# A decoder step's stalls: rope's copies first, low parts moved between engines, and later weights, gates and taps

## The chip, the cores and the metric

The kernel runs on one core of one Trainium2 chip. A core has five engines, each with its own instruction queue: TensorE (PE: matmuls; PEld: its weight loads), VectorE (DVE), ScalarE (ACT), GpSimd (POOL), and SyncE (SP), which here starts all DMA transfers. They share the on-chip memory SBUF; matmuls write to PSUM. The metric is the time of one execution in microseconds (us), as the median of three runs.

## The reference

One layer of a decoder with three parallel branches, for a prompt of 1024 positions and 8 samples of 4 positions (together 1056 columns), in float32:

```python
h = rmsnorm(x, norm_mix_g)
q, k, v, g, su, sv, xq, gt = split(h @ w_in)
o_ret, S = retention(rope(q), rope(k), v, silu(g))        # 4 heads, group norm
o_sg  = gelu(su) * (tril(sg_ws) @ layernorm(gelu(sv)) + sg_bs)
o_x   = softmax(xq @ mk.T) @ mv                           # 256 memory tokens
merged = sig(gA) * (o_ret @ w_br_ret) + sig(gB) * (o_sg @ w_br_sg) + sig(gC) * (o_x @ w_br_x)
x = x + merged @ w_o
z = rmsnorm(x, norm_ffn_g) @ w_up                         # 1024 -> 2 x 2816
a, b = split(conv_b + causal depthwise convolution of width 3 over z)
x = x + (gelu(a) * b) @ w_down
y = rmsnorm(x, norm_final_g)
```

Model width is 1024. States of the retention and the convolution and the normalised gate rows are returned too.

## The kernel before, in words

Activations lie feature-major: a tile is 128 features by 1056 columns. Each matmul is computed in three terms: both operands are split into a high part (rounded to float32r) and a low part (the rest), and high x high, high x low and low x high are summed in PSUM.

Weights come as slabs of 128 x 1024 (the list SLABS gives their order). `w_prep` makes one ready: its DMA lands in wr, ScalarE casts it to wh (whs in the down projection), and GpSimd subtracts to get wl (wls); for the slabs in the set LO_DVE, VectorE subtracts instead (`vtt` is VectorE's two-tensor operation, `ptt` is GpSimd's). There are three buffers of wh and wl. `w_ahead` calls `w_prep` if a buffer is free.

A unit `fm` computes one output tile of 128 features in 8 k-steps of nine matmuls (three terms by three column chunks), into one PSUM tile, mp. After each k-step it calls `hook`. A hook pops functions due from the list `wait` (filled by `later(n, fn)`: run fn n hooks from now), one entry of a side list, and, by a `rate` of steps per hook, advances generators that hold secondary work: norms, the retention, attention, convolutions. Every engine works off its queue in the order in which the code issues; that order is set by these hooks and rates, written by hand. An instruction that reads a PSUM tile is also ordered behind earlier readers of it.

The places that the change touches:

- **Start.** `xnorm` sums the squares of x (tiles xr) over k = 4 to 7 on ScalarE, YA hooks after it begins, adds them on VectorE, and `rstd_all` splits the sum into rsh and rsl, sums over features with matmuls (ap<-rsh, ap<-rsl) and forms rst. Meanwhile q and k of head 0 are projected together, and the silu gate behind them needs rst.
- **Rope.** `rope_evac` takes q's or k's PSUM tile: VectorE multiplies by the cosines, ScalarE copies the two halves swapped into sw, GpSimd multiplies sw by sines, and VectorE adds. In heads 1 to 3 this falls among the retention of the head before, whose group norm uses GpSimd for a tiny reciprocal root (grs) between VectorE's mv and cB; ort follows from them.
- **Spatial gate and cross-attention.** su, sgt and sgS belong to the spatial gate. In cross-attention, KS splits a head's cached keys (kch, kcl), QS its queries (xqh, xql), XA to YC are scores, softmax and products (xt, pt).
- **Gates.** `gate` projects one tile of a gate; calling what it returns runs the tanh (th) and stores it.
- **Output projection.** wo runs in two halves of 528 columns, eight slabs each (L1534 calls `w_ahead`). During the second half the first is normalised (ns, nst, rst, `h_scale` into x2c, xl) and sums of up weights (fs) are formed.
- **Up projection.** The up projection's second pair uses 2x2 products; `z_put` assembles z, and a convolution has `first`, `tap(1)`, `tap(0)`, `gelu`.
- **Down projection.** Groups of two slabs; in each, eight outputs m of 18 matmuls are added to x; the last convolution's steps run at `rate[0]` per output. acl is an activation's low part.
- **Tail.** The last two groups are computed by column chunks of 512, 288 and 256 (c = 0, 1, 2). `fin_evac` adds to x, squares (sq), and adds to ssf; `fin(c)` casts ssf to sy, sums over features (ap<-sy), gets rsy, and multiplies into y; `fin_last` does it for c = 2, where the squares of m = 6, 7 go straight into float32 matmuls.

In the program `H` is 4, `NFF` 22, `NUP` 44.

Of the kernel before, what the change touches and what calls it, by code (L numbers as in the profile page):

```python
# [75 lines left out]

LO_DVE = [k for i, k in enumerate(SLABS) if k[0] in ("km", "vm") and i % 2] + [("sv", 0, 0), ("sv", 0, 1)]


@with_exitstack  # L80
def step_kernel(ctx: ExitStack, tc: tile.TileContext, xT, memT, wslab, cst, ident_d, rope, vec, sgc, sgm, sgs,
# [10 lines left out]
    def slot(name, dt=F32, shape=None):  # L92
        return sp.tile(shape or [P, T], dt, tag="S", name=name, bufs=NSLOT)
# [31 lines left out]
    def psv(ps):  # L125
        return [ps[:, 0:2, 0:384], ps[:, 2, 0:288]]

    def seg(t):
        return [t[:, 0:768].rearrange("p (a b) -> p a b", a=2), t[:, 768:1056]]
# [101 lines left out]
    def fm(key, ops, kbase=0, free=True):  # L231
        hi, lo = w_get(key)
        hv = hi.rearrange("p (k c) -> p k c", c=P)
        lv = lo.rearrange("p (k c) -> p k c", c=P)
        ps = mp()
        n = len(ops)
        for k in range(n):
            rh, rl = ops[k]
            for i, (a, r) in enumerate(((hv, rh), (hv, rl), (lv, rh))):
                for c, (c0, w) in enumerate(CH):  # L240
                    mm(ps[:, c, 0:w], a[:, kbase + k, :], r[:, c0:c0 + w],
                       start=(k == 0 and i == 0), stop=(k == n - 1 and i == 2))
            if k == 0 or k == 3:
                w_ahead()
            hook()
        if free:
            w_free(key)
        return ps
# [107 lines left out]
    with tc.manual_schedule():  # L356
# [72 lines left out]

        YA, YB = 14, 3  # L430

# [43 lines left out]
        def rope_evac(ps, name):  # L475
            sw = slot("sw")
            out = slot(name)
            for o, i, c in zip(seg(out), psv(ps), seg(cosT)):
                vtt(o, i, c, ALU.mult)
            for (a, b) in ((0, 64), (64, 0)):  # L480
                for o, i in zip(seg(sw), psv(ps)):
                    nc.scalar.copy(out=o[a:a + 64], in_=i[b:b + 64])
            ptt(sw, sw, sinT, ALU.mult)
            later(4, lambda: vtt(out, out, sw, ALU.add))
            return out
# [459 lines left out]
        def xattn(h):  # L945
# [134 lines left out]
            for fn, *a in ((XA, 0), (YA, 0), (XA, 1), (YA, 1), (XB, 0), (VS, 0), (XB, 1), (XC, 0), (VS, 1), (XA, 2), (YB,),  # L1080
                           (XC, 1), (XB, 2), (XA, 3), (YC, 0), (XC, 2), (KS, h + 1, 0), (XB, 3), (YC, 1),
                           (KS, h + 1, 1), (XC, 3), (QS, h + 1), (YD,)):
                while defer:
                    defer.pop(0)()
                fn(*a)
                if fn not in (VS, KS, QS):
                    yield
# [211 lines left out]
        for m in range(8):  # L1299
            if m == 6:  # L1300
                side.extend([g_load] * 8)
            if m == 7:
                side.extend([lambda k=k: g_scale(k) for k in range(8)])
            gate(("gb", m))()
        drain()
# [430 lines left out]
        vtt(za[1][:, :, 2:6], za[1][:, :, 2:6], by4(u4[:, 2 * HA:HW]), ALU.add)  # L1736
        pb.first()
        pb.tap(1)
        conv = [Conv(1, *za), Conv(NFF + 1, *zb)]
        n = prod(d["a22"], "T4", tick=do)  # L1740
        z_put(n, 0, *zb, u3)
        pb.tap(0)
        conv_end(0, pa, pb)
# [98 lines left out]
        gens.append(last_conv())  # L1842
        rate[0] = 1.0

# [19 lines left out]
        def down(g):  # L1864
            ws = dn_get(g)
            tr = terms(g, ws)
            for m in range(8):
# [4 lines left out]
                for o, i in zip(seg(x2t[m]), psv(ps)):  # L1872
                    vtt(o, o, i, ALU.add)
                if m in (1, 3, 5):
                    w_ahead()
# [15 lines left out]
        rsy = slot("rsy")  # L1891
        sy3 = slot("sy3", F32R)
        FCH = ((0, 512), (512, 288), (800, 256))

        def fin(c):
            c0, w = FCH[c]
            r = rsy[:, c0:c0 + w]
            yield
            yield from rstd_cols(ssf[:, c0:c0 + w], w, r, sy3, fine=True)
            for m in range(0, 8, 2):  # L1900
                y = slot("y", shape=[P, 2, 512])
                for i in range(2):
                    ptt(y[:, i, 0:w], x2t[m + i][:, c0:c0 + w], r, ALU.mult)
                later(2, lambda m=m, y=y: dma(yT[m:m + 2, :, c0:c0 + w].rearrange("m p t -> p m t"), y[:, :, 0:w]))
                yield

        def fin_last(sqs):
# [3 lines left out]
            a = ap()[:, 0:w]  # L1911
            mm(a, ones, sy3[:, 0:w], stop=False)
            mm(a, ones, sy3[:, w:2 * w], start=False, stop=False)
            for i in range(2):
                mm(a, f(ones), sqs[i], start=False, stop=(i == 1))
            t = slot("rn")
# [19 lines left out]
        def fin_evac(c, us, pss):  # L1936
# [8 lines left out]
            for m in us:  # L1945
                if c == 2 and m > 5:
                    last_sq.append(sqs[m])
                elif m:
                    vtt(ssf[:, sl], ssf[:, sl], sqs[m], ALU.add)
            if c == 2 and us[-1] == 5:  # L1950
                nc.scalar.copy(out=sy3[:, 0:w], in_=ssf[:, sl])
                vtt(sy3[:, w:2 * w], ssf[:, sl], f(sy3[:, 0:w]), ALU.subtract)
            for m in us:
# [176 lines left out]
```

## Time and profile before

| | us |
|---|---|
| median of three runs | 1917.12 (1916.0 to 1917.32) |
| the profiled execution | 1916.06 |
| its span, first to last instruction | 1913.9 |
| TensorE busy | 1854.7 |
| VectorE busy | 1144.7 |
| GpSimd busy | 921.5 |
| ScalarE busy | 651.8 |

The mean clock that TensorE was granted is 0.991 of full. Of the 2.2 us between the span and the execution's time nothing is seen in the trace. Rows of instructions read: start in us, duration in us, engine, line of the code, operation, out<-in, shapes, count, and in brackets the engine's idle time before it and what ended that. The count x3 means three instructions one behind the other, with one duration from the start of the first to the end of the last. Rows of waits read: the instructions that waited, what they waited for, then the sum in us, how often, and the longest.

### The profile page before, as it was taken

How to read it: one execution, taken by the hardware profiler on the slowest of the kernel's cores; microseconds unless marked ns; L12 is line 12 of the kernel's file. 1: busy time of each engine (PE TensorE's matmuls, PEld its weight loads, DVE VectorE, ACT ScalarE, POOL GpSimd, SP SyncE). 2: the span in 40 equal slices, each digit the busy share in tenths (PEclk: the TensorE clock that was granted, in tenths of full speed). 3: DMA queues.
4: the chain of work that ended last, by engine and by line, in shares of the span. 5: the costliest groups of instructions: out<-in, count | busy, mean ns of one | idle time of the engine just before them, and what ended most of it. 6: DMA issues, size and time to landing. Idle time of an engine off the chain costs nothing.

```text
span 1913.9 us, 32100 instructions
## 1 busy us (share of the span) xinstructions
PE 1854.7 (97%) x13369; PEld 1828.0 (96%) x13369; DVE 1144.7 (60%) x1610; ACT 651.8 (34%) x1016; POOL 921.5 (48%) x583
## 2 busy tenths in 40 slices
PE   8899999999999999999999999899999999999997
PEld 8899999999999998999999999899999999999996
DVE  6554545442464479332352267999999999744447
ACT  6333232421233434323211233544344344321204
POOL 2243434221643421555544533577777777754404
PEclk9999999999999999999999999999999999999998
DMA  5112131324133341426632532022222223732202
GB/s 189 54 45 93 44 105 36 132 66 156 56 135 112 124 181 55 135 90 255 241 124 79 189 140 84 34 90 79 68 90 79 67 90 120 252 133 90 76 1 91
DMA packets 59808, 204.82 MB, mean 107 GB/s; under 512 B 6608, under 2 KB 9840, under 8 KB 59664
## 3 DMA queue, kind: packets, MB, share of 16 engines
q1 hardware_dynamic: 59664, 202.78, 30.8%
q8 instruction: 105, 1.72, 0.4%
q14 instruction: 39, 0.32, 0.1%
HBM read 154.34 MB, written 48.41 MB: 106 GB/s over the span
## 4 chain that ended last, share of the span: by engine, by line
PE 50%; DVE 7%; issue 1%; ACT 1%; POOL 1%; DMA 1%; DVEq 0%; SPq 0%; POOLq 0%; ACTq 0%
PE bp L108 25%; PE mp L108 25%; DVE c L120 1%; DVE xl L114 1%; DVE x2c L120 1%; DVE fs L114 1%; DVE ssf L114 0%; DMA opr<-scr 0%; POOL opl L117 0%; DMA wr<-in_wslab 0%; DVE x L114 0%; ACT xh L1153 0%; DVE hx L114 0%; POOL acl L117 0%; POOL wls L117 0%
## 5 line engine op out<-in xcount | busy, mean ns | idle before, releaser
L117 POOL TENSOR_TENSOR wl<-wr,wh 128x1024 fp32r<-128x1024 f32 x107 | 282.7, 2645 | 438.3 <-ACT wh L152 294.7
L108 PE MATMUL bp<-xh,wh 128*128 128x264 f32 (+1 forms) x1376 | 279.2, 284 | 6.8 <-DVE th L114 2.4
L108 PE MATMUL bp<-xh,wl 128*128 128x264 f32 (+1 forms) x1376 | 280.3, 285 | 1.2 <-POOL wl L117 0.7
L108 PE MATMUL bp<-xl,wh 128*128 128x264 f32 (+1 forms) x1376 | 279.8, 285 | 0.0
L108 PEld LDWEIGHTS bp<-xh,wh 128*128 128x128 f32 x1376 | 215.0, 189 | 8.2 <-issue 3.1
L108 PEld LDWEIGHTS bp<-xh,wl 128*128 128x128 f32 x1376 | 215.0, 189 | 1.8 <-POOL wl L117 1.2
L108 PEld LDWEIGHTS bp<-xl,wh 128*128 128x128 f32 x1376 | 214.5, 189 | 0.0
L108 PE MATMUL mp<-hh,wh 128*128 128x384 f32 (+1 forms) x816 | 190.0, 340 | 4.9 <-ACT hh L111 4.8
L108 PE MATMUL mp<-hl,wh 128*128 128x384 f32 (+1 forms) x816 | 179.6, 327 | 0.3 <-DVE hl L120 0.3
L114 DVE TENSOR_TENSOR x<-x,mp 128x288 f32<-128x288 f32 (+3 forms) x167 | 105.7, 676 | 120.6 <-PE mp L108 120.6
L108 PE MATMUL mp<-hh,wl 128*128 128x384 f32 (+1 forms) x816 | 177.6, 324 | 0.0
L117 POOL TENSOR_TENSOR wl<-fs,wh 128x1024 fp32r<-128x1024 f32 x52 | 146.2, 2814 | 50.9 <-ACT wh L1179 50.4
L108 PEld LDWEIGHTS mp<-hh,wh 128*128 128x128 f32 x816 | 136.0, 191 | 7.8 <-ACT hh L111 5.4
L108 PEld LDWEIGHTS mp<-hl,wh 128*128 128x128 f32 x816 | 136.6, 190 | 1.1 <-DVE hl L120 1.0
L108 PEld LDWEIGHTS mp<-hh,wl 128*128 128x128 f32 x816 | 137.0, 189 | 0.0
L108 PE MATMUL mp<-ach,whs 128*128 128x384 f32 (+3 forms) x524 | 124.3, 326 | 4.0 <-DVE x L114 3.1
L120 DVE SCALAR_TENSOR_TENSOR c<-z,hist,c 128x1024 f32<-128x1024 f32 x88 | 125.0, 1420 | 4.3 <-ACT c L111 4.2
L108 PE MATMUL mp<-ach,wls 128*128 128x384 f32 (+3 forms) x524 | 123.7, 325 | 0.0
L108 PE MATMUL mp<-acl,whs 128*128 128x384 f32 (+3 forms) x524 | 123.4, 325 | 0.0
L152 ACT CAST wh<-wr 128x1024 fp32r<-128x1024 f32 x86 | 89.4, 1043 | 95.8 <-PE mp L108 54.2
L1179 ACT CAST wh<-fs 128x1024 fp32r<-128x1024 f32 x55 | 57.7, 1050 | 155.6 <-DVE fs L114 145.3
L120 DVE SCALAR_TENSOR_TENSOR c<-zs,hist,c 128x32 f32<-128x32 f32 x88 | 110.6, 1256 | 0.0
(367 smaller groups left out, 4161.5 us busy)
## 6 DMA issues: line engine op xcount, KB each, us to landing
wr<-in_wslab SPq DMA_DIRECT2D x162, 512.0 KB, 3.7
sg<-th SPq DMA_DIRECT2D x24, 528.0 KB, 5.2
th<-sg SPq DMA_DIRECT2D x24, 528.0 KB, 5.5
sca<-c SPq DMA_DIRECT2D x22, 528.0 KB, 3.0
opr<-sca SPq DMA_DIRECT2D x22, 528.0 KB, 4.7
opr<-scr SPq DMA_DIRECT2D x16, 528.0 KB, 7.0
scr<-ort SPq DMA_DIRECT2D x8, 528.0 KB, 7.6
hx<-in_xT SPq DMA_DIRECT2D x8, 528.0 KB, 5.9
```

Source lines behind the costliest of these rows:

```text
L108: nc.tensor.matmul(out=out, lhsT=l, rhs=r, start=start, stop=stop)
L114: nc.vector.tensor_tensor(out=out, in0=a, in1=b, op=op)
L117: nc.gpsimd.tensor_tensor(out=out, in0=a, in1=b, op=op)
L120: nc.vector.scalar_tensor_tensor(out=out, in0=a, scalar=s, in1=b, op0=op0, op1=op1)
L152: nc.scalar.copy(out=hi, in_=raw)
L1179: nc.scalar.copy(out=hi, in_=src)
```

## The change

- `LO_DVE` also holds the second half of wo and xq 2 and 3: their low parts are made by VectorE.
- `fm` calls `w_ahead` after its second and fifth k-step instead of the first and fourth.
- At the start, YA is 11 instead of 14. `rope_evac` copies sw before the multiplication in head 0; in the other heads GpSimd's multiplication is issued two hooks later, and the addition five hooks later instead of four.
- In cross-attention the next head's QS comes before its second KS.
- The tanh and store of gate gb run two hooks later.
- In the up projection's second pair `first` and `tap(1)` come behind the last `z_put`.
- In the down groups the rate is 0.34 instead of 1, and group 0 has no `w_ahead` at m = 1.
- In the tail, chunk 1 begins its norm two hooks later; four y of chunk 0 are VectorE's; chunk 2 casts ssf into a tile of its own, sy4, after m = 2, and the squares of m = 3 to 7 go into float32 matmuls.

```diff
 LO_DVE = [k for i, k in enumerate(SLABS) if k[0] in ("km", "vm") and i % 2] + [("sv", 0, 0), ("sv", 0, 1)]
+LO_DVE += [("wo", m, 1) for m in range(8)]
+LO_DVE += [("xq", 2), ("xq", 3)]
...
-            if k == 0 or k == 3:
+            if k == 1 or k == 4:
                 w_ahead()
...
-        YA, YB = 14, 3
+        YA, YB = 11, 3
...
         def rope_evac(ps, name):
             sw = slot("sw")
             out = slot(name)
+            def turn():
+                for (a, b) in ((0, 64), (64, 0)):
+                    for o, i in zip(seg(sw), psv(ps)):
+                        nc.scalar.copy(out=o[a:a + 64], in_=i[b:b + 64])
+
+            if h == 0:
+                turn()
             for o, i, c in zip(seg(out), psv(ps), seg(cosT)):
                 vtt(o, i, c, ALU.mult)
-            for (a, b) in ((0, 64), (64, 0)):
-                for o, i in zip(seg(sw), psv(ps)):
-                    nc.scalar.copy(out=o[a:a + 64], in_=i[b:b + 64])
-            ptt(sw, sw, sinT, ALU.mult)
-            later(4, lambda: vtt(out, out, sw, ALU.add))
+            if h:
+                turn()
+            if h:
+                later(2, lambda: ptt(sw, sw, sinT, ALU.mult))
+            else:
+                ptt(sw, sw, sinT, ALU.mult)
+            later(5 if h else 4, lambda: vtt(out, out, sw, ALU.add))
             return out
...
-                           (KS, h + 1, 1), (XC, 3), (QS, h + 1), (YD,)):
+                           (QS, h + 1), (KS, h + 1, 1), (XC, 3), (YD,)):
...
-            gate(("gb", m))()
+            later(2, gate(("gb", m)))
...
-        pb.first()
-        pb.tap(1)
         conv = [Conv(1, *za), Conv(NFF + 1, *zb)]
         n = prod(d["a22"], "T4", tick=do)
         z_put(n, 0, *zb, u3)
+        pb.first()
+        pb.tap(1)
         pb.tap(0)
...
         gens.append(last_conv())
-        rate[0] = 1.0
+        rate[0] = 0.34
...
-                if m in (1, 3, 5):
+                if m in ((3, 5) if g == 0 else (1, 3, 5)):
                     w_ahead()
...
-        sy3 = slot("sy3", F32R)
+        sy3, sy4 = slot("sy3", F32R), slot("sy4", F32R)
...
-            yield
+            for _ in range(3 if c else 1):
+                yield
             yield from rstd_cols(ssf[:, c0:c0 + w], w, r, sy3, fine=True)
...
-                    ptt(y[:, i, 0:w], x2t[m + i][:, c0:c0 + w], r, ALU.mult)
+                    (vtt if c == 0 and m < 4 else ptt)(y[:, i, 0:w], x2t[m + i][:, c0:c0 + w], r, ALU.mult)
...
-            mm(a, ones, sy3[:, 0:w], stop=False)
-            mm(a, ones, sy3[:, w:2 * w], start=False, stop=False)
-            for i in range(2):
-                mm(a, f(ones), sqs[i], start=False, stop=(i == 1))
+            mm(a, ones, sy4[:, 0:w], stop=False)
+            mm(a, ones, sy4[:, w:2 * w], start=False, stop=False)
+            for i in range(len(sqs)):
+                mm(a, f(ones), sqs[i], start=False, stop=(i == len(sqs) - 1))
...
-                if c == 2 and m > 5:
+                if c == 2 and m > 2:
                     last_sq.append(sqs[m])
...
-            if c == 2 and us[-1] == 5:
-                nc.scalar.copy(out=sy3[:, 0:w], in_=ssf[:, sl])
-                vtt(sy3[:, w:2 * w], ssf[:, sl], f(sy3[:, 0:w]), ALU.subtract)
+            if c == 2 and us[-1] == 2:
+                nc.scalar.copy(out=sy4[:, 0:w], in_=ssf[:, sl])
+                vtt(sy4[:, w:2 * w], ssf[:, sl], f(sy4[:, 0:w]), ALU.subtract)
```

The changed program's line numbers are some two higher near the helpers. On ScalarE, at the start of the program, from q's last copies sw to the cast rsh, before (xr<-xr are the squares, two pairs):

```order
L482 COPY sw<-mp 64x768
L482 COPY sw<-mp 64x288
L152 CAST wh<-wr 128x1024
L111 ACTIVATE xr<-xr 128x1056 x2
L482 COPY sw<-mp 64x768
L482 COPY sw<-mp 64x288
L482 COPY sw<-mp 64x768
L482 COPY sw<-mp 64x288
L152 CAST wh<-wr 128x1024
L111 ACTIVATE xr<-xr 128x1056 x2
L337 CAST rsh<-xr 128x1056
```

On ScalarE from the same copies to the same cast, now:

```order
L483 COPY sw<-mp 64x768
L483 COPY sw<-mp 64x288
L154 CAST wh<-wr 128x1024
L113 ACTIVATE xr<-xr 128x1056 x2
L483 COPY sw<-mp 64x768
L483 COPY sw<-mp 64x288
L483 COPY sw<-mp 64x768
L483 COPY sw<-mp 64x288
L154 CAST wh<-wr 128x1024
L339 CAST rsh<-xr 128x1056
```

The pair that stands here now is the second; the first stands ahead of q's copies, and nothing but a weight's cast is left between k's copies and rsh.

On GpSimd, in head 2's rope of k among the retention of head 1 (grs are the group norm's two small operations), before:

```order
L117 TENSOR_TENSOR grs<-mv,cB 128x1
L117 TENSOR_TENSOR grs<-grs,nhalf 128x1
L117 TENSOR_TENSOR sw<-sw,sinT 128x1056
L117 TENSOR_TENSOR wl<-wr,wh 128x1024
L117 TENSOR_TENSOR grs<-mv,cB 128x1
L117 TENSOR_TENSOR grs<-grs,nhalf 128x1
```

On GpSimd at the same place, now:

```order
L119 TENSOR_TENSOR grs<-mv,cB 128x1
L119 TENSOR_TENSOR grs<-grs,nhalf 128x1
L119 TENSOR_TENSOR grs<-mv,cB 128x1
L119 TENSOR_TENSOR grs<-grs,nhalf 128x1
L119 TENSOR_TENSOR wl<-wr,wh 128x1024
L119 TENSOR_TENSOR sw<-sw,sinT 128x1056
```

The second pair of grs moved ahead of sw and wl, and sw moved behind wl.

On VectorE, in the second half of wo, from one output's addition to the next (x2c<-mp,x2c adds an output, fs are sums of up weights), before:

```order
L120 SCALAR_TENSOR_TENSOR x2c<-mp,x2c 128x528
L114 TENSOR_TENSOR ssq<-ssq,sq 128x528
L114 TENSOR_TENSOR fs<-fr 128x512
L114 TENSOR_TENSOR fs<-fs,fr 128x512
L120 SCALAR_TENSOR_TENSOR x2c<-x2c,vecs,rst 128x528
L114 TENSOR_TENSOR xl<-x2c,xh 128x528
L120 SCALAR_TENSOR_TENSOR x2c<-x2c,vecs,rst 128x528
L114 TENSOR_TENSOR xl<-x2c,xh 128x528
L120 SCALAR_TENSOR_TENSOR x2c<-mp,x2c 128x528
```

On VectorE at the same place, now:

```order
L122 SCALAR_TENSOR_TENSOR x2c<-mp,x2c 128x528
L116 TENSOR_TENSOR ssq<-ssq,sq 128x528
L116 TENSOR_TENSOR fs<-fr 128x512
L116 TENSOR_TENSOR fs<-fs,fr 128x512
L116 TENSOR_TENSOR wl<-wr,wh 128x1024
L122 SCALAR_TENSOR_TENSOR x2c<-x2c,vecs,rst 128x528
L116 TENSOR_TENSOR xl<-x2c,xh 128x528
L122 SCALAR_TENSOR_TENSOR x2c<-x2c,vecs,rst 128x528
L116 TENSOR_TENSOR xl<-x2c,xh 128x528
L122 SCALAR_TENSOR_TENSOR x2c<-mp,x2c 128x528
```

One wl per output came in ahead of the next addition; it was GpSimd's before.

## The prediction

> **What bounds the kernel now.** I read the page's busy times first, then the list of TensorE's waits, then busy time and granted clock in the stretches where the long waits lie, and last the rows of the engines that end those waits.
>
> ```profile
> PE 1854.7 (97%) x13369; PEld 1828.0 (96%) x13369; DVE 1144.7 (60%) x1610; ACT 651.8 (34%) x1016; POOL 921.5 (48%) x583
> ```
>
> TensorE is the bound: of the span of 1913.9 us it leaves 59.2 idle. A change that leaves its matmuls alone (this one adds three small ones at the end) can win those 59 us and what a reduced clock costs, no more. The first column after the colon is the sum in us, then how often, then the longest:
>
> ```profile
> PE ap L108 <- ACT rsh L337: 5.9, 1, 5.9
> ...
> PE ap L108 <- DVE ort L120: 3.7, 3, 2.9
> PE mp L108 <- DVE x L114: 3.1, 2, 2.6
> PE ap L108 <- DVE sgt L114: 3.0, 1, 3.0
> PE mp L108 <- DVE x2c L120: 2.7, 2, 2.0
> ...
> PE bp L108 <- DVE z L114: 2.1, 1, 2.1
> PE ap L108 <- DVE xql L114: 2.1, 1, 2.1
> PE ap L108 <- ACT sy L319: 1.9, 1, 1.9
> PE ap L108 <- DVE ns L114: 1.7, 1, 1.7
> PE ap L108 <- DVE pt L114: 1.6, 3, 0.9
> PE mp L108 <- DVE silu L114: 1.5, 1, 1.5
> PE ap L108 <- ACT xt L111: 1.3, 1, 1.3
> ...
> PE bp L108 <- POOL wl L117: 0.7, 1, 0.7
> ```
>
> Nearly every row is one wait at one place, and each part of the change touches one of these places. The last row says that weights are practically never late. The stretches (PEclk is the granted clock):
>
> ```profile
> core 0: us, PE busy (x) PEld busy (x) DVE busy (x) ACT busy (x) POOL busy (x), PEclk, DMA share, GB/s
> 45.00:56.00 11.00, 4.51 (x15) 3.98 (x15) 7.74 (x6) 3.88 (x4) 5.17 (x13) 0.69 0.23 54
> 223.00:230.00 7.00, 4.06 (x18) 3.63 (x17) 3.83 (x8) 0.47 (x1) 2.40 (x3) 0.76 0.25 75
> 527.00:534.00 7.00, 4.04 (x18) 3.76 (x18) 6.74 (x7) 0.00 (x0) 2.21 (x1) 0.76 0.74 235
> 593.00:597.00 4.00, 3.60 (x25) 3.57 (x26) 2.59 (x8) 1.02 (x4) 0.00 (x0) 1.00 0.90 259
> 1120.00:1160.00 40.00, 35.62 (x277) 35.04 (x276) 34.87 (x36) 16.53 (x24) 15.51 (x6) 0.96 0.30 100
> 1227.00:1245.00 18.00, 14.79 (x107) 14.40 (x106) 17.93 (x21) 6.73 (x13) 9.37 (x11) 0.91 0.17 60
> 1653.00:1660.00 7.00, 4.41 (x19) 4.16 (x18) 7.00 (x7) 2.02 (x2) 7.00 (x3) 0.76 0.58 181
> 1888.00:1896.00 8.00, 5.56 (x32) 5.15 (x31) 7.00 (x12) 3.56 (x9) 6.54 (x5) 0.79 0.47 176
> ```
>
> A long wait is paid twice: in 223 to 230 the mean clock is 0.76, so (1-0.76) x 7.00 = 1.7 us of TensorE's time is lost to the clock after a wait of 2.9; 1.7 again after sgt and x, 1.7 after sy, 1.6 after x2c (0.04 x 40) and z (0.09 x 18). After xql (2.1, stretch 593 to 597) the clock stays 1.00: the wait must lie badly for it. I count 1.5 for each window, since part of one is idle.
>
> The Trainium skill ("TensorE: Matmul & The Clock Gate", Why this matters for your kernels) asks only that idle gaps between matmuls stay under about 3 us; by it, only the 5.9 us wait would cost clock here, and the sum below would be smaller by five windows x 1.5 = 7.5 us. The stretches above, with waits of 1.9 to 3.0 us and a clock of 0.76 to 0.79, speak against it, and I go by them.
>
> **Part by part** (gains positive).
>
> *Start.*
>
> ```profile
> 29.53 2.19 ACT L482 COPY sw<-mp 64x768 f32<-64x768 f32 x4 [5.15 <-DVE q L114]
> 32.70 2.06 ACT L111 ACTIVATE xr<-xr 128x1056 f32<-128x1056 f32 x2
> 44.34 5.52 DVE L114 TENSOR_TENSOR xr<-xr 128x1056 f32<-128x1056 f32 x3 [4.19 <-ACT xr L111]
> 55.91 0.64 PE L108 MATMUL mp<-hh,wh 128*128 128x384 f32 x3
> 56.39 0.65 PE L108 MATMUL mp<-hl,wh 128*128 128x384 f32 x3
> ```
>
> The squares of the first norm wait on ScalarE behind the rope copies sw, and these wait for VectorE's multiplication q, though they need only the PSUM tile. The change lets the first pair of squares run in the 5.15 that ScalarE idled, and copies before it multiplies, so that sw starts at about 27.7 (an estimate: 29.53 less the multiplication). The second pair followed sw's start by 32.70 - 29.53 = 3.17, so it runs from 30.9 to 33.0. xr's three sums, 1.84 each beside GpSimd (5.52 / 3), end at 38.5, the cast rsh (1.1) at 39.6; rsl stands behind k's multiplication and q's addition on VectorE (together 2.5), and ends at 42.3 (40.8 to 43.5).
>
> TensorE's summing matmuls stand three k-steps earlier. A k-step is three triples, 3 x (56.39 - 55.91) = 1.45, so they come at about 40.7 instead of 45.1, where the wait began (51.0 - 5.9). The copies now hold the multiplication up, but its tile is needed again only two outputs later. So 5.9, 1.5 (silu, which the same chain makes late) and 2.0 of clock go: in 45 to 56 the clock lost (1-0.69) x 11.00 = 3.4, part of it while TensorE stood. Of the 9.4, a new wait of 0 to 2.5, taken as 1.4, comes back. Gain 8 (6 to 10).
>
> *Rope in heads 1 to 3.*
>
> ```profile
> 219.90 2.47 POOL L117 TENSOR_TENSOR sw<-sw,sinT 128x1056 f32<-128x1056 f32 x1 [4.66 <-ACT sw L482]
> 222.31 2.39 POOL L117 TENSOR_TENSOR wl<-wr,wh 128x1024 fp32r<-128x1024 f32 x1
> 224.64 0.21 POOL L117 TENSOR_TENSOR grs<-mv,cB 128x1 f32<-128x1 f32 x1
> ```
>
> The group norm's tiny grs stands behind sw and wl on GpSimd; behind it on VectorE wait cB and ort, and TensorE 2.9 for ort. In head 2 grs now stands ahead of both: 2.9 + 1.5 clock = 4.4. In heads 1 and 3 the second grs stays behind both, and wl starts later, its cast now behind the copies: grs about 1.1 us later, 0.8 lost in each (0 to 2). Gain 2.8 (0.4 to 4.4).
>
> *xq's low parts on VectorE.*
>
> ```profile
> 523.79 5.98 DVE L114 TENSOR_TENSOR su<-su,sgt 128x512 f32<-128x512 f32 x1
> 524.54 4.67 POOL L117 TENSOR_TENSOR wl<-wr,wh 128x1024 fp32r<-128x1024 f32 x2
> L114 DVE TENSOR_TENSOR wl<-fs,wh x3: 1225/1226/1256, 728.3 to 764.0; 128x1024 fp32r<-128x1024 f32 x3
> ```
>
> A VectorE operation on two SBUF tiles that meets one on GpSimd lasts until that is done: su took 5.98. With both wl on VectorE, at 1.23 each as the last row shows for such tiles, su meets none, but a wl of 1.23 may stand ahead of the next sgt: that follows about 2 us earlier. The wait of 3.0 shrinks to 0.9, the clock window goes: gain 3.5 (1 to 4.5).
>
> The Trainium skill ("Perfetto Trace Analysis", Optimizing Scalar/DVE Operations) warns that VectorE and GpSimd share a port, so moving operations between these two might not help; by it this term and wo's below would be 0, and the sum 6.5 smaller. The rows have a price for both sides, 1.23 on VectorE against a wait of 2.4 per wl, so I keep the terms, and make the warning a rival.
>
> *QS ahead of the second KS.* xqh's cast moves ahead of another tile's; xql, for which TensorE waits 2.1 without loss of clock, is ready before it is needed. Gain 2.0 (1 to 2.1). The key halves behind it come one step later; they are used a head later.
>
> *gb gates two hooks later.*
>
> ```profile
> 695.83 1.18 ACT L111 ACTIVATE th<-th,vecs 128x1056 f32<-128x1056 f32 x1 [4.14 <-DVE th L114]
> ```
>
> In this stage the attention of the xq heads runs between the gates' k-steps, and a gate's tanh of 1.18 stands ahead of pt's casts and xt's exponentials on ScalarE. Behind them it delays only its own store on SP's queue, which is read back a stage later. The waits for xt (1.3) and pt (1.6) are the ones it can shorten: 2.9 at best; since other casts stay ahead of them, I take half. Gain 1.5 (0 to 2.9).
>
> *wo's second half, low parts on VectorE.*
>
> ```profile
> 1122.27 2.45 DVE L114 TENSOR_TENSOR ns<-ssq,ns 128x528 fp32r<-128x528 f32 x1 [0.76 <-ACT ns L1476]
> ```
>
> ns took 2.45 because a wl ran on GpSimd. Without the eight wl's there, ns' wait of 1.7 shrinks to 0.6, x2c's 2.7 to 1.0, and the window's 1.5 goes: 4.3. But VectorE is busy 34.87 of 40 here, and gets 8 x 1.23 = 9.8 for the locked time it loses, and a wl stands ahead of ns. I take 3.0 (-1 to 6).
>
> *Second up pair.* z is written 1.3 earlier, but VectorE is busy 17.93 of 18 in that stretch, so what TensorE gains on z it waits for at zu. -0.4 (-2 to 1.5).
>
> *Down groups.* Taps at 0.34 per hook instead of 1: VectorE, full from 1653 to 1660 (7.00 of 7.00), has x earlier. The 3.1 and the window's 1.5 go; three taps that meet GpSimd's low parts leave about 0.35 each, and one weight less ahead costs nothing, as the row for wl in the waits says (if that cover is gone, one slab's 2.4). Gain 3.6 (1 to 4.6).
>
> *Tail.*
>
> ```profile
> 1884.10 3.71 DVE L114 TENSOR_TENSOR ssf<-ssf,sq 128x288 f32<-128x288 f32 x3
> 1897.21 6.86 POOL L117 TENSOR_TENSOR y<-x,rsy 128x288 f32<-128x288 f32 x8 [2.67 <-DVE rsy L120]
> 1899.37 2.36 DVE L114 TENSOR_TENSOR ssf<-ssf,sq 128x256 f32<-128x256 f32 x3
> ```
>
> The column sum's two matmuls of chunk 1 now stand 30 matmuls later, among chunk 2's second group, so sy's wait of 1.9 and its window go, 3.4. Ahead of that sy, though, VectorE gets four y of 0.7 to 1.2 (the ssf additions beside GpSimd took 3.71 / 3), of which about 1.5 comes back as a rest of the wait. In the last group the additions (2.36) leave the path for three pairs of small matmuls beside x: some 1.5 more. Against it, rsy of chunk 1 comes behind x of chunk 2, so GpSimd's eight y (6.86) now run beside the last norm and the last six y on VectorE and stretch them, or end last themselves, about 2. Left are 3.4 - 1.5 + 1.5 - 2 = 1.4, taken as 1.5 (-2 to 4.5).
>
> The sum: 8 + 2.8 + 3.5 + 2.0 + 1.5 + 3.0 - 0.4 + 3.6 + 1.5 = 25.5. A removed wait uncovers another: behind the 5.9 stood 1.5 (silu). I take 3 off, an eighth, for those the rows do not show yet. 22.5 against the profiled execution's own 1916.06 gives 1893.6; the median stands 1.06 higher: 1894.6.
>
> **Rivals.**
>
> *Shared-port swaps give nothing.* wo, xq and the tail only exchange a wait on GpSimd for work on VectorE, and each window stays. Then 3.0 + 3.5 + 1.5 is missing: a gain of 14.5, 1902.6. For it: VectorE's 34.87 of 40; against it: su's 5.98, of which two wl of 1.23 would use 2.5. This is the case of the warning in the Trainium skill's "Perfetto Trace Analysis" above.
>
> *Rests still trip the clock.* At four places (start, wo, down, tail) a wait near 1.9 remains and the window with it: 4 x (1.5 + 0.5) = 8 lost (0.5 for the longer rest), 1902.6 likewise. Against it: 2.1 for xql tripped nothing.
>
> *Nothing uncovered, and the ends reached.* Without the 3 taken off, and with the upper ends of start (2 more) and wo (3 more): 1917.1 - 25.5 - 5 = 1886.6. For it: most waits stand alone, microseconds from the next; against it: silu behind rsh.
>
> *Slower: weights late.* Every feature-major unit now prepares its next weights one k-step (1.45 us) later.
>
> ```profile
> L117 POOL TENSOR_TENSOR wl<-wr,wh 128x1024 fp32r<-128x1024 f32 x107 | 282.7, 2645 | 438.3 <-ACT wh L152 294.7
> ```
>
> If the low part were the last thing that a unit waits for, each of the 56 units (56 calls over the loops of heads, gates and branches) would lose up to 1.45. At 22.5 / 56 = 0.40 each it takes all that the rest wins, and at 0.5 each the time is 1894.6 + 28 = 1922.6. Against it: TensorE waited for wl 0.7 us in all, and GpSimd idled 438.3 ahead of those 107.
>
> **How the numbers follow.** Forecast (1887 to 1901) 0.64; swaps give nothing 0.13; rests trip the clock 0.08; the better ends 0.07; slower 0.04; nearly nothing left, by several new waits of the size of the old, 0.04. The time is the forecast's. The range reaches to 1886.5 below, the better end, and to 1904 above, just past the two rivals at 1902.6. 0.2% is 3.8 us, about what a measurement of this kernel tells from no change. Faster 0.93, same 0.03, slower 0.04.
>
> **What would show it.** rsh's wait under 2.5; ort, sgt, xql, x at 1657 and sy gone from the long waits, and clock 1.00 in those stretches; su at 0.7 to 2; ns at 0.7; TensorE's idle time near 37 us, not 59. The prediction is wrong if wl or wh appear among TensorE's waits with more than 5 us, if x2c or zu wait longer than 3, or if GpSimd's y is the last work.

## The result, and the profile after

The changed kernel takes 1896.23 us (median of four runs, 1894.87 to 1897.33) against 1916.56 for the kernel before (median of four); the ratio is 0.9894, 95% interval 0.9877 to 0.9911. The forecast was 1894.6, range 1886.5 to 1904.0. The profiled execution took 1896.17 with a span of 1894.2, 19.7 less than before.

The page's busy times after:

```profile
PE 1845.7 (97%) x13375; PEld 1821.7 (96%) x13375; DVE 1137.5 (60%) x1621; ACT 652.0 (34%) x1016; POOL 906.1 (48%) x569
```

TensorE stands idle 48.5 us instead of 59.2, and its busy time fell by 9.0 with six matmul records more (two for each of the three small matmuls): that part is clock, not work. The mean granted clock rose from 0.991 to 0.995. TensorE's waits after:

```profile
PE mp L110 <- DVE x L116: 5.2, 4, 1.6
PE ap L110 <- ACT rsh L339: 3.2, 1, 3.2
PE ap L110 <- DVE ort L122: 2.9, 2, 1.5
...
PE bp L110 <- DVE zt L116: 2.3, 1, 2.3
PE ap L110 <- DVE rsl L116: 1.8, 1, 1.8
PE mp L110 <- DVE x2c L122: 1.3, 2, 0.9
...
PE bp L110 <- POOL wl L119: 0.7, 1, 0.7
...
PE ap L110 <- DVE ns L116: 0.5, 1, 0.5
...
PE ap L110 <- ACT sy L321: 0.2, 1, 0.2
...
PE ap L110 <- DVE sgt L116: 0.2, 1, 0.2
```

xql is gone from the list, sgt, sy and ns shrank to 0.5 or less; ort's 2.9 is two waits of 1.5 and 1.4 instead of one long one, zt's 2.3 is new, and rsh and rsl still stand for 5.0. Stretches of the same stages after, with the granted clock in the column PEclk:

```profile
41.00:56.00 15.00, 10.28 (x49) 9.88 (x50) 10.76 (x11) 6.24 (x7) 2.85 (x2) 0.77 0.14 37
...
210.00:230.00 20.00, 20.00 (x133) 19.59 (x132) 14.35 (x29) 5.19 (x10) 7.00 (x8) 1.00 0.09 27
520.00:534.00 14.00, 13.77 (x100) 13.38 (x99) 13.46 (x18) 2.14 (x3) 3.82 (x2) 1.00 0.58 193
1105.00:1145.00 40.00, 38.15 (x310) 37.56 (x309) 32.35 (x43) 18.72 (x26) 3.90 (x2) 1.00 0.34 110
1205.00:1227.00 22.00, 18.35 (x132) 17.51 (x131) 21.93 (x22) 9.56 (x18) 13.20 (x12) 0.92 0.18 71
1630.00:1640.00 10.00, 10.00 (x64) 10.00 (x63) 7.77 (x11) 4.93 (x5) 6.59 (x4) 1.00 0.32 107
...
1865.00:1878.00 13.00, 10.31 (x81) 9.46 (x80) 10.79 (x21) 6.44 (x16) 5.08 (x4) 1.00 0.44 163
```

Five of the seven stretches of reduced clock are whole; the start (0.77) and the up pair (0.92) are not. Where the time came from is read by matching each matmul with itself in the other trace. Its start before less its start after is TensorE's lead there, in us:

| before the matmul at (us, before) | lead | gained in the stage | forecast |
|---|---|---|---|
| 72.0, behind the start | 1.6 | 1.6 | 8 |
| 399.9, behind heads 1 to 3 | 4.1 | 2.5 | 2.8 |
| 560.0, behind the spatial gate | 8.1 | 4.0 | 3.5 |
| 759.6, behind attention and gb | 14.9 | 6.8 | 3.5 |
| 1180.0, behind wo | 18.9 | 4.0 | 3.0 |
| 1300.1, behind the second up pair | 18.2 | -0.7 | -0.4 |
| 1870.1, behind the down groups (lead 18.0 at 1610) | 19.5 | 1.5 | 3.6 |
| end of the span | 19.7 | 0.2 | 1.5 |

A lead also moves where nothing was changed. The first matmul starts anywhere from 4.8 to 5.7. The seven traces with the changed kernel's start (its own, e4, e5, e6, e8, e9, e12) lie up to 1.0 apart at 70 us; two of the experiments (e8, e12) lost 1.2 in the up pair, and one (e6) 1.8 in the down groups, without an edit there. In the experiments, too, a lead is that of one trace over another, and a cost is the change of the lead across the stage that was edited. Spans are of one profiled execution each, unless an interval is given; the changed kernel's is 1894.2, and its four executions have 1892.9 to 1895.4.

### The profile page after: what moved, and what is told of

It reads as the page before. It is cut to its first block, busy times and chain, and to the rows that moved or that the text cites. A ratio compares the mean times of both kernels' runs of the same rounds, so it can differ in the third digit from the quotient of the medians.

```text
span 1894.2 us, 32097 instructions
## 1 busy us (share of the span) xinstructions
PE 1845.7 (97%) x13375; PEld 1821.7 (96%) x13375; DVE 1137.5 (60%) x1621; ACT 652.0 (34%) x1016; POOL 906.1 (48%) x569
## 4 chain that ended last, share of the span: by engine, by line
PE 52%; DVE 7%; ACT 1%; issue 1%; POOL 1%; DVEq 0%; ACTq 0%
PE bp L110 26%; PE mp L110 25%; DVE c L122 2%; DVE xl L116 1%; DVE x2c L122 1%; DVE fs L116 0%; DVE wl L116 0%; DVE x L116 0%; DVE hx L116 0%; POOL opl L119 0%; DVE z L116 0%; ACT xh L1164 0%; DVE ssf L116 0%; DVE c L116 0%; ACT sq L113 0%
## 5 line engine op out<-in xcount | busy, mean ns | idle before, releaser
L119 POOL TENSOR_TENSOR wl<-wr,wh 128x1024 fp32r<-128x1024 f32 x97 | 258.4, 2666 | 424.6 <-ACT wh L154 284.6
```

Of the source, the lines that this page charges most:

```text
L119: nc.gpsimd.tensor_tensor(out=out, in0=a, in1=b, op=op)
```

## The experiments

### Where the start's gain went

The first undoes the start alone.

```diff
-        YA, YB = 11, 3
+        YA, YB = 14, 3
...
-            if h == 0:
-                turn()
             for o, i, c in zip(seg(out), psv(ps), seg(cosT)):
                 vtt(o, i, c, ALU.mult)
-            if h:
-                turn()
+            turn()
```

> The changed kernel with the start as before (YA 14, copies behind the multiplication in head 0). Theory A (the start part gave little, since the three additions of xr now lie beside four GpSimd operations in a row and took 9.77 us instead of 5.52): the three waits at the start are 5.9, 0.6 and 1.5 again, TensorE is 1.5 to 2.5 us later from 70 us on than in the changed kernel, and the span is about 1896 (1894.2 + 1.6 to 2.5). Rival B (the start part is worth the 8 us forecast, and something else in the changed kernel, such as the weights prepared a k-step later, loses 6 there): TensorE is some 8 us later from 70 us on, span about 1902.

The waits at the start were 5.9, 0.6 and 1.5 again, TensorE was 2.4 later at 70 us, and the span was 1896.9. Theory A stands: the start was worth 2.4 in this pair of traces and not 8. (Set against all seven traces with the new start, the kernel before and e1 give 0.7 to 2.4.) The rows of VectorE and then of GpSimd in the changed kernel show why:

```profile
33.02 9.77 DVE L116 TENSOR_TENSOR xr<-xr 128x1056 f32<-128x1056 f32 x3 [1.72 <-ACT xr L113]
...
32.45 2.41 POOL L119 TENSOR_TENSOR wl<-wr,wh 128x1024 fp32r<-128x1024 f32 x1
35.28 3.05 POOL L119 TENSOR_TENSOR sw<-sw,sinT 128x1056 f32<-128x1056 f32 x1 [0.41 <-ACT sw L483]
38.28 3.38 POOL L119 TENSOR_TENSOR wl<-wr,wh 128x1024 fp32r<-128x1024 f32 x1
```

The three additions begin at 33.0, as forecast, but each lies beside one of GpSimd's operations, and they take 2.96, 3.43 and 3.31: 9.77 for three, where the forecast took the 5.52 of before. Of those 5.52 only the first addition lay beside GpSimd, and this is its row:

```profile
44.34 2.93 DVE L114 TENSOR_TENSOR xr<-xr 128x1056 f32<-128x1056 f32 x1 [4.19 <-ACT xr L111]
```

The other two took 1.26 each. If so, taking one operation off GpSimd must bring rsh forward.

```diff
+LO_DVE += [("g", 1)]
```

> The changed kernel with one more low part made by VectorE: that of the silu gate's second slab, the first of the two that GpSimd makes beside the additions of xr. Theory A: GpSimd's row then has the two sw and one wl, the additions start beside nothing, the last ends with the second sw at about 37.8, rsh at about 39; TensorE's wait of 3.2 for rsh goes, that for rsl (1.8) shrinks under 1, the clock stays 1.00: 5 to 7 us less, span 1887 to 1889. Rival B (the squares and copies set rsh, not GpSimd): rsh comes at most 1 us earlier and the span stays within 1.5 us of 1894.2.

VectorE, then TensorE, in this run:

```profile
33.89 5.99 DVE L117 TENSOR_TENSOR xr<-xr 128x1056 f32<-128x1056 f32 x3
39.80 1.31 DVE L117 TENSOR_TENSOR k<-mp,cosT 128x768 f32<-128x768 f32 x2
41.03 2.20 DVE L117 TENSOR_TENSOR q<-q,sw 128x1056 f32<-128x1056 f32 x1
...
44.45 0.45 PE L111 MATMUL ap<-rsl,ones 128*128 128x384 f32 x1 [2.97 <-DVE rsl L117]
```

The additions take 5.99 (1.24, 1.26 and, beside sw, 3.42), the wait for rsh is gone, the clock stays at 1.00 from 40 to 50 us, and the span is 1889.9, 4.3 less. The mechanism of A is shown; the size fell short of 5, because rsl, behind q's addition (2.20, stretched as well), now waits 3.0 and not under 1. Moving the next slab's low part as well helps no more:

```diff
+LO_DVE += [("g", 1), ("v", 0, 0)]
```

> As the run before, and the next slab's low part (v of head 0) also by VectorE, where it stands ahead of rsl. Theory A: additions as before or shorter by up to 1 us, rsh at 39 or earlier, but rsl about 1.2 later than in the run before, so a wait of 1 to 2 for rsl: span 0 to 2 us above that run's. Rival B: the span stays within 1.5 us of 1894.2.

Span 1892.0, 2.1 above e2, of which 1.0 stands from the first matmuls on. The low part stands ahead of rsl, whose wait is 3.2 and not the 1 to 2 of theory A, and in 41 to 56 the clock is 0.89, where e2 has 1.00.

### The rope, and the weights a k-step later

```diff
-            if h:
+            if h == 2:
                 later(2, lambda: ptt(sw, sw, sinT, ALU.mult))
...
-            later(5 if h else 4, lambda: vtt(out, out, sw, ALU.add))
+            later(5 if h == 2 else 4, lambda: vtt(out, out, sw, ALU.add))
```

> The changed kernel with sw's multiplication and the addition put off in head 2 alone; heads 1 and 3 as before. Theory A (putting off helps where grs stood behind sw, and loses 1.0 and 1.1 in heads 1 and 3, where it still stands behind wl, which starts later): the waits for ort in heads 1 and 3 are about 0.4 instead of 1.5 and 1.4, head 2 has none, span 2.1 lower, about 1892. Rival B (weights prepared a k-step later make the 1.5 in heads 1 and 3, whatever sw does): both waits stay at 1.4 to 1.5 and the span at 1894.

The waits for ort in heads 1 and 3 did fall to 0.4 and 0.3, but a wait for st of 0.7 and 0.9 appeared earlier in each, where sw now delays another norm. The lead over the changed kernel changed by less than 0.2 in each head, and the span is 1894.1: A was right on ort and wrong on the sum. Then the step of the weights alone was undone:

```diff
-            if k == 1 or k == 4:
+            if k == 0 or k == 3:
                 w_ahead()
```

> The changed kernel with weights prepared after the first and fourth k-step again. Theory A (the shift costs nothing, since weights are ready long ahead, and wins a little where it puts a cast behind others on ScalarE): span 0 to 2.5 higher, no wait for wl over 1 us in either. Rival B (the later weights cost in heads 1 and 3, where grs waits behind a wl that starts later): the waits for ort in heads 1 and 3 fall from 1.5 and 1.4 to about 0.4, span about 2 lower.

Both theories fell: the span is 1905.6, 11.4 more. TensorE is 1.3 later at 110 us, 3.1 at 140, 10.6 at 240, 12.4 at 400 and 13.1 at 560; from there to 700 it makes up 1.7. So nearly all of it is lost in heads 1 to 3. ort is waited for 2.1, 4.0 and 2.0, and the clock is 0.77 over 225 to 240:

```profile
PE ap L110 <- DVE ort L122: 8.1, 3, 4.0
```

ScalarE, GpSimd and VectorE in head 2 of that run:

```profile
223.35 1.05 ACT L154 CAST wh<-wr 128x1024 fp32r<-128x1024 f32 x1
224.30 0.36 ACT L538 COPY cB<-ap 128x256 f32<-128x256 f32 x1
...
224.47 2.38 POOL L119 TENSOR_TENSOR wl<-wr,wh 128x1024 fp32r<-128x1024 f32 x1 [5.73 <-ACT wh L154]
226.81 0.19 POOL L119 TENSOR_TENSOR grs<-mv,cB 128x1 f32<-128x1 f32 x1
227.08 0.55 POOL L119 TENSOR_TENSOR grs<-grs,nhalf 128x1 f32<-128x1 f32 x1
227.59 2.40 POOL L119 TENSOR_TENSOR sw<-sw,sinT 128x1056 f32<-128x1056 f32 x1
...
227.66 2.48 DVE L541 TENSOR_SCALAR cB<-cB,mv,grs 128x256 f32<-128x256 f32 x1 [5.75 <-POOL grs L119]
```

Without the later step the cast wh is issued ahead of the norm's copy cB, so that wl stands ahead of grs on GpSimd. sw, put off by two hooks, now starts just when VectorE uses grs, and stretches that operation as well (2.48). In the changed kernel the same operation takes 0.41, and wl and sw follow it:

```profile
220.31 0.41 DVE L541 TENSOR_SCALAR cB<-cB,mv,grs 128x256 f32<-128x256 f32 x1 [1.91 <-ACT cB L538]
221.24 2.39 POOL L119 TENSOR_TENSOR wl<-wr,wh 128x1024 fp32r<-128x1024 f32 x1 [1.95 <-ACT wh L154]
```

The later cast is not a neutral edit: it takes wl from in front of the norm. Is it enough by itself? One run had the rope of heads 1 to 3 as before, with the weights kept later, and three edits elsewhere:

```diff
+LO_DVE += [("g", 1)]
...
-            if h:
-                later(2, lambda: ptt(sw, sw, sinT, ALU.mult))
-            else:
+            if 1:
                 ptt(sw, sw, sinT, ALU.mult)
-            later(5 if h else 4, lambda: vtt(out, out, sw, ALU.add))
+            later(4 if h else 7, lambda: vtt(out, out, sw, ALU.add))
...
-        rate[0] = 0.34
+        rate[0] = 0.25
```

> The changed kernel with the silu gate's second low part by VectorE (as in e2), q's addition in head 0 put behind rsl (7 hooks instead of 4), the rope of heads 1 to 3 as before the change (with the weights still prepared a k-step later), and taps at 0.25 per output in the down groups. Theory A, start: rsl ends 1 to 1.5 sooner than in e2, where q's addition of 2.2 stood ahead of it, so 1 to 1.5 more than e2's 4.2. Theory A, rope: the later weights alone take wl out of the group norm's way in head 2 (ScalarE's copy of cB goes ahead of the cast), and sw's move adds nothing there: head 2's wait for ort stays under 0.6, heads 1 and 3 as in e4, so the same time within 0.5. Rival B, rope: sw's 2.5 ahead of grs is what counts, the wait in head 2 is 2 or more, and with a reduced clock 2 to 4 are lost there. Down groups: at 0.25 one tap less lies beside GpSimd's low parts, 0 to 1.5 earlier at 1690. Span under theory A 1887 to 1889.5.

Rope: rival B holds. GpSimd, VectorE and TensorE in head 2:

```profile
216.98 2.46 POOL L120 TENSOR_TENSOR sw<-sw,sinT 128x1056 f32<-128x1056 f32 x1 [4.66 <-ACT sw L484]
219.39 0.19 POOL L120 TENSOR_TENSOR grs<-mv,cB 128x1 f32<-128x1 f32 x1
219.66 0.55 POOL L120 TENSOR_TENSOR grs<-grs,nhalf 128x1 f32<-128x1 f32 x1
220.18 2.35 POOL L120 TENSOR_TENSOR wl<-wr,wh 128x1024 fp32r<-128x1024 f32 x1
...
220.25 2.43 DVE L540 TENSOR_SCALAR cB<-cB,mv,grs 128x256 f32<-128x256 f32 x1 [4.77 <-POOL grs L120]
...
223.61 0.59 PE L111 MATMUL ap<-V,rt 128*128 128x256 f32 x3 [2.70 <-DVE ort L123]
```

Now grs stands ahead of wl, but behind sw, and wl stretches cB in its turn; TensorE loses 4.0 over the three heads. The waits for ort or st in heads 1, 2, 3 side by side:

| | rope as before | sw put off |
|---|---|---|
| weights as before | 0.4, 2.9, 0.4 (before) | 2.1, 4.0, 2.0 (e7) |
| weights a k-step later | 0.7, 0.7 + 2.7, 0.7 (e10) | 1.5, 0, 1.4 (changed) |

Neither half gains alone; together they do. In TensorE's time over the three heads, against the kernel before, sw put off alone loses 8.7, the later weights alone lose 1.4, and both gain 2.5. In the same run, q's addition behind rsl took rsl's wait from 3.0 (e2) to 1.8, but the clock over 40 to 50 is 0.83, where e2 has 1.00, and the lead over the changed kernel at 70 us is 3.2 against e2's 3.8: the 1 to 1.5 of theory A are not there. Taps at 0.25 lost 0.2 between 1610 and 1700, no more than runs differ by there: one wait of 2.0 with a reduced clock (0.83 over 1650 to 1660) stands where the changed kernel has 1.2 and 1.6 without.

### Cross-attention: QS and the gates

```diff
-                           (QS, h + 1), (KS, h + 1, 1), (XC, 3), (YD,)):
+                           (KS, h + 1, 1), (XC, 3), (QS, h + 1), (YD,)):
```

> The changed kernel with QS behind the second KS again. The stretch of cross-attention gained 6.6 us in the changed kernel (TensorE 8.2 us earlier at 573 us, 14.8 at 703). Theory A (QS gave 2.8 of it, at 590, the gates' delay the rest): the wait for xql of 2 to 3 us comes back, TensorE is 2.0 to 3.0 later from there, span 1896.2 to 1897.2. Rival B (the delayed gates alone gave it, since they free ScalarE for xqh's cast): no wait for xql, span within 0.6 of 1894.2.

```diff
-            later(2, gate(("gb", m)))
+            gate(("gb", m))()
```

> The changed kernel with the gb gates' tanh and store issued at once, as before. Theory A (the delay gave the 3.8 us by which TensorE got ahead between 600 and 703, in steps of 0.4 to 1.2 at pt, xt and kch): TensorE is 3 to 4 later at 703, span 1897 to 1898; waits for pt, ys and xt come back. Rival B (QS's move and the weights' later casts gave part): 1 to 2 later, span 1895 to 1896.

With QS back TensorE is 1.1 later at 700 us, but it is 1.0 later at 70 and at 550 already, ahead of the edit. So QS back cost 0.1, without any wait for xql: rival B. With the tanh at once TensorE is 0.6 later at 550 and 1.8 at 700: a cost of 1.2, rival B's size. The span is 1896.8, but 1.8 of its 2.6 come in only at 1648, in the down groups, where the edit changes nothing in the order: a wait for x of 2.7 instead of 1.2. That part is not the gates'. The next run undoes both; its expectation still takes the two costs as 1.0 and 1.9, without what stood ahead of the edits:

> The changed kernel with both cross-attention edits undone: QS behind the second KS, and the gates' tanh at once. Alone, QS cost 1.0 at 600 us and 0.7 in the span, the gates' tanh 1.9 at 700. Theory A (they stand in for each other: either one frees ScalarE early enough for xqh's cast): together they cost more than the sum of 2.9, namely 4.5 to 7, with the wait for xql of about 2 us back, TensorE 4.5 to 7 later at 703 us. Rival B (independent): 2.5 to 3.3 later at 703, no wait for xql over 1.

TensorE was 0.1 later at 550 and 2.6 at 700, the span is 1896.6, and the wait for xql was 0.2. That lies within rival B's bounds, but these rested on the 2.9. Alone the two cost 0.1 and 1.2, together 2.5, so in part they do stand in for each other: of the three runs only this one waits long for y (0.7 twice, at 586 and 626 us). The two gave 2.5 of the 6.8 in this stretch. The long wait for xql stays away without QS's move (here), and also with it when the weights are prepared a step earlier (e7). What removed it here is seen on ScalarE. First before, then e12, which has the same order of QS, KS and gates:

```profile
587.67 1.18 ACT L111 ACTIVATE th<-th,vecs 128x1056 f32<-128x1056 f32 x1 [1.24 <-DVE th L114]
588.75 1.03 ACT L152 CAST wh<-wr 128x1024 fp32r<-128x1024 f32 x1
589.69 1.07 ACT L293 CAST xqh<-xq 128x1056 fp32r<-128x1056 f32 x1
...
590.79 2.55 DVE L114 TENSOR_TENSOR xql<-xq,xqh 128x1056 fp32r<-128x1056 f32 x1 [3.15 <-ACT xqh L293]
```

```profile
579.53 1.18 ACT L113 ACTIVATE th<-th,vecs 128x1056 f32<-128x1056 f32 x1 [1.25 <-DVE th L116]
580.62 1.06 ACT L295 CAST xqh<-xq 128x1056 fp32r<-128x1056 f32 x1
581.58 1.04 ACT L154 CAST wh<-wr 128x1024 fp32r<-128x1024 f32 x1
...
581.71 1.26 DVE L116 TENSOR_TENSOR xql<-xq,xqh 128x1056 fp32r<-128x1056 f32 x1 [2.21 <-ACT xqh L295]
```

The weight's cast moved behind xqh: again the k-step. With wl not yet on GpSimd, xql takes 1.26, not 2.55. This is read from the order of the casts; no run undoes the k-step with QS back. The k-step also costs 1.7 in this stretch, between 670 and 700 us: e7, and the mended version below, gain that much there by undoing it. The rest of the 6.8 is not told apart; the low parts of xq on VectorE were not undone alone.

### wo's low parts

```diff
-LO_DVE += [("wo", m, 1) for m in range(8)]
```

> The changed kernel with the low parts of wo's second half by GpSimd again. Theory A (VectorE pays 1.2 a piece and is spared the longer wait for GpSimd): the waits for ns (1.7) and x2c (2.7 in two) return with a stretch of reduced clock, TensorE is 3.5 to 4.5 later at 1175 us than in the changed kernel, span 1897.7 to 1898.7. Rival B (an exchange without gain; the 4.1 us came from other parts, for instance weights prepared later): 0 to 1.5 later, span 1894 to 1896.

The waits are back as theory A has them:

```profile
PE mp L109 <- DVE x2c L121: 2.7, 2, 2.0
...
PE ap L109 <- DVE ns L115: 1.7, 1, 1.7
```

Between 1100 and 1145 us TensorE loses 2.9, under theory A's 3.5 to 4.5 and well over rival B's 1.5; the span is 1897.9, and the rest of its 3.7 arose where the edit changes nothing. The missing 1 of the 4.0 fits the clock: here it stayed 1.00 after the wait of 2.0, which before brought a reduced stretch. Rival B is out: the exchange pays. In the changed kernel ns takes 0.70 (2.45 before), and in the spatial gate the first su takes 1.06 (5.98 before):

```profile
1108.03 0.70 DVE L116 TENSOR_TENSOR ns<-ssq,ns 128x528 fp32r<-128x528 f32 x1
520.92 1.06 DVE L116 TENSOR_TENSOR su<-su,sgt 128x512 f32<-128x512 f32 x1
```

### Up pair, down groups and tail, each undone in one run

```diff
+        pb.first()
+        pb.tap(1)
         conv = [Conv(1, *za), Conv(NFF + 1, *zb)]
         n = prod(d["a22"], "T4", tick=do)
         z_put(n, 0, *zb, u3)
-        pb.first()
-        pb.tap(1)
...
-        rate[0] = 0.34
+        rate[0] = 1.0
...
-                    (vtt if c == 0 and m < 4 else ptt)(y[:, i, 0:w], x2t[m + i][:, c0:c0 + w], r, ALU.mult)
+                    ptt(y[:, i, 0:w], x2t[m + i][:, c0:c0 + w], r, ALU.mult)
```

> The changed kernel with three parts undone at three places that lie far apart, so that TensorE's lead at each can be read by itself: the taps ahead of the last z_put in the second up pair, the rate 1.0 in the down groups, and all y of the first chunk by GpSimd. Theory A: up pair 0.6 earlier at 1245 us than the changed kernel (the wait for z of 2.1 and its reduced clock come back, but the 3.4 lost behind it do not); down groups 1.5 to 3 later at 1690 (TensorE waits for x longer than 1.2 and 1.6); tail 1.5 to 2.5 earlier by 1875 (the waits of 1.6 and 0.7 for x go, since VectorE's y of 2.4 and 1.3 stood ahead of them), but the span only 0 to 1.5 shorter for it, as GpSimd has y until 1876 in any case. Rival B: the new waits in the down groups come from the missing weight ahead, not from taps (rate 1.0 then changes under 0.7 there), and the tail is set by sy, so that y on GpSimd locks VectorE's additions and loses 1 to 2.

Up pair: 0.6 earlier at 1245, as A says; the taps' new place loses. Down groups: 1.9 lost between 1610 and 1700, with one wait of 2.6 at 1638 and a clock of 0.83 over 1635 to 1645. So the gain there goes with the rate, as theory A has it, and not with the missing weight. It does not come in every execution: e6 lost 1.8 at the same place with the rate at 0.34, while nine other traces with that rate lie between -0.1 and 0.8 of the changed kernel's. The changed kernel's own waits of 1.2 and 1.6 come from taps that last as long as GpSimd's low parts beside them; here are a tap's small part alone, then GpSimd's low parts and the same small part beside them:

```profile
1633.56 0.24 DVE L122 SCALAR_TENSOR_TENSOR c<-zs,hist,c 128x32 f32<-128x32 f32 x1
...
1651.30 5.74 POOL L119 TENSOR_TENSOR wls<-wr,whs 128x1024 fp32r<-128x1024 f32 x2
...
1652.37 2.39 DVE L122 SCALAR_TENSOR_TENSOR c<-zs,hist,c 128x32 f32<-128x32 f32 x1
```

Tail: the waits for x went and TensorE gained 2.9 by 1874, but then sy, whose additions lay beside GpSimd's y for longer, took it all back and 1.0 more; the span is 1896.2:

```profile
1876.86 0.55 PE L110 MATMUL ap<-sy,ones 128*128 128x288 f32 x1 [2.76 <-ACT sy L321]
```

Rival B holds in the tail: y on VectorE costs two waits of 2.3 in all and saves one of 2.8 with its clock (0.83 over 1874 to 1884).

### A mended version

```diff
+LO_DVE += [("g", 1)]
...
-            if k == 1 or k == 4:
+            if k in ((1, 4) if key[0] in ("q", "k", "g", "su") else (0, 3)):
...
+        pb.first()
+        pb.tap(1)
         conv = [Conv(1, *za), Conv(NFF + 1, *zb)]
...
-        pb.first()
-        pb.tap(1)
```

> The changed kernel with three mends: the silu gate's second low part by VectorE (4.3 us in e2), the taps of the second up pair ahead of the last z_put again (0.6 in e9), and weights prepared after the first and fourth k-step again from cross-attention on, with the later steps kept in the heads' units and the spatial gate (in e7 TensorE made up about 1.5 between 570 and 700 us). Theory A: these add up, as they lie apart: 5 to 6.5 us under the changed kernel, span 1887.7 to 1889.2, time about 1889.7 to 1891.2, ratio to the kernel before 0.986. Rival B: only e2's part stands, as the small ones are of the size by which one run differs from another: time 1891.5 to 1893.

The median is 1892.46 (1890.69 to 1893.83), the ratio to the kernel before 0.9873, 95% interval 0.9856 to 0.9889; the profiled execution, the fastest of the four, has a span of 1888.9. By that one trace theory A holds: it is 5.3 under the changed kernel's, with a lead of 3.5 at 70 us, 0.6 lost in the spatial gate, 1.7 gained by 700 and 0.6 in the up pair. By the median rival B holds: 1892.46 lies within its 1891.5 to 1893, 3.8 under the changed kernel's median and not under e2's single execution (1891.68), and the two intervals overlap. So it is not shown that the mends add up to more than e2's.

## Why the prediction was right, and which terms were not

- **Start (8, came 1.6 to 2.4).** The failed step is "xr's three sums, 1.84 each beside GpSimd (5.52 / 3)". Of the three only one lay beside GpSimd in the rows before (2.93); the other two took 1.26 each. Moved earlier, all three met an operation of GpSimd, and took 9.77, so rsh was cast at 42.8 and not at 38.5, and its wait stayed at 3.2. The additions' beginning at 33.0, sw at 27.7 and TensorE's arrival at 40.7 (came 40.8) were right. The clock loss stayed: 0.77 over 41 to 56, in both kernels.
- **Rope (2.8, came 2.5).** The effect was right, its reason half: head 2 gained 4.5 and heads 1 and 3 lost 1.0 each. But the later cast, weighed only as a cost in heads 1 and 3, is one half of the gain in head 2.
- **Weights a k-step later.** The prediction made this the slower rival, at 0.5 per unit. That loss did not come: wl is still waited for 0.7 in all. But the step decides which ScalarE and GpSimd operation a cast and wl stand ahead of. Undoing it costs 11.4, since the rope's move needs it, and it costs 1.7 itself in cross-attention. That a shift can hurt or help through a neighbour was weighed in heads 1 and 3 alone.
- **xq (3.5, came 4.0) and wo (3.0, came 4.0; 2.9 without the clock).** The rival "shared-port swaps give nothing" is out: with wo it was tried by itself, in the tail putting y back on GpSimd lost 1.0 (e9), and with xq it is only read from the lead and from su's row.
- **QS and gates (3.5 together, came 2.5 of the stretch's 6.8).** xql's wait was put down to QS alone. It stays away without QS's move too (e12), where the later weights have put a cast behind xqh; beside them QS's move is worth 0.1, not 2.0. Some 2 of the 6.8 have no run that shows their cause.
- **Up pair (-0.4, came -0.7).** Its mechanism was right, but its place was not: z's wait shrank from 2.1 to 0.8, and one of 2.3 with a reduced clock (0.92) took its place at zt, not at zu.
- **Down (3.6, came 1.5).** The mis-sized term is "three taps leave about 0.35 each": two of them left 1.2 and 1.6, so x's waits fell only from 3.1 to 2.8, and the rest of the gain is clock.
- **Tail (1.5, came 0.2).** sy's wait and its window went, but the rest, taken as 1.5, was 1.6 + 0.7 for x, ahead of which the y stand. TensorE gained 1.9 in the tail, where the terms ahead of its end make 3.4. Behind its last matmul 1.7 were lost, since GpSimd's ten y stretched the last norm on VectorE; the prediction took off about 2 for that.
- **The 3 taken off for waits uncovered.** Terms came 5.6 below their sum of 25.5, not 3 below: the total was near in part by luck, because errors of -6.4 (start) and +3.3 (attention) stand against each other, not because each term was right. "TensorE's idle time near 37" was wrong too (48.5), as 9 of the 19.7 came by the clock.

## What to carry to other kernels

When a VectorE operation is moved, price it by what GpSimd does at the new time, not by its old duration. When a prefetch is shifted by one step, look in the order of every engine it uses for the neighbour that it now stands behind or ahead of: the prefetch may be early enough either way, and still decide who waits. Undo each part alone, and read the lead of one trace over the other stage by stage, less the lead that stood ahead of the edit. Here that showed that more than half of the result is lost without an edit that was costed at nothing, because another edit needs it.

## What the runs showed of the hardware that was not expected

VectorE is also held up by GpSimd in an operation with one tile input and per-partition scalars (cB: 2.43 to 2.48 beside GpSimd, 0.41 in the changed kernel, without), not only in one on two tiles; with a PSUM input (k, 1.31 beside a wl) it isn't. And the length of a wait does not say whether the clock falls: 2.97 (e2), 2.70 (e10) and 2.0 (e8) left it at 1.00, while 2.0 (e10, down groups), 2.3 (zt) and 2.6 (e9) brought 0.79 to 0.83 over the stretches of 8 to 10 us around them. The Trainium skill ("TensorE: Matmul & The Clock Gate", Part 1, What's actually happening) says that the monitor's window of 3413 ns runs free of the program; that fits waits that count only by where they fall in it, so that a shift at one place can change the price of a wait at another. No run here moves one wait alone to show it.
